# Splitting w_out into two parts during the last k, v and q projections, by way of a DRAM scratch

## The chip, the cores and the metric

The kernel runs on one core of one Trainium2 chip. The metric is the time of one execution on the device in microseconds; the figure before is the median of three runs. The profile is of one further execution. Engines are named as the profile names them: PE is TensorE (PEld its weight loads), DVE is VectorE, ACT is ScalarE, POOL is GpSimd, SP is the engine whose queue issues nearly all DMAs here. Times within an execution are counted from the start of the profile's span.

## The reference

One layer of an encoder for two sequences (256 and 2048 tokens, each with 16 meta tokens ahead; 1024 channels). One input projection is cut into attention (q, k, v, gate) and convolution (value, gate, SiLU gate); both results are gated, joined, and go through one output projection:

```python
h = rmsnorm(z, norm_w)
proj = jnp.einsum('bld,de->ble', h, w_in)
q, k, v, g_att, c_val, c_glu, g_conv = jnp.split(proj, SPLIT_IDX, axis=-1)
...
att = windowed_gqa(q, k, v, sink).reshape(B, L, W_ATT) * jax.nn.silu(g_att)
cnv = conformer_conv(c_val, c_glu, conv_w, conv_b, ln_w, ln_b) * jax.nn.silu(g_conv)
mixed = jnp.concatenate([att, cnv], axis=-1)
return z + jnp.einsum('ble,ed->bld', mixed, w_out)
```

Everything is float32. w_out is 1024 x 1024, 4 MB.

## The kernel before

**Precision.** Matmuls run in float32r. To keep float32 accuracy each operand is split into two parts: hi is the value cast to float32r, lo is the rest (value minus hi). A product takes three matmuls, hi by hi, hi by lo and lo by hi (PASSES, L125). The split of a tile is a cast on ACT and a subtraction on another engine.

**Phase one, the projections.** Tokens come in 18 blocks of 128 and in 6 groups of 3 blocks; the groups form two chunks (c = 0 and c = 1). w_in is cut into 11 units of 256 columns. For each chunk the units are run in the order of ORDER (L965): four convolution units, two gates of the convolution, two gates of attention, k and v together (kv_group), and two units of q (q_group). In chunk 0 a unit's weights are loaded raw into tiles with the tag wraw (pool sp, four buffers of 2 KB per partition), split, and the two parts are stored in the DRAM scratch wd; in chunk 1 units 2 and up are loaded from wd in two parts (L720 to L724). So the wraw buffers are last used early in chunk 1's weight preparation. The results of phase one go to DRAM scratches (qd, kd, vd, gd), the convolution with its LayerNorm (ln_block) runs beside it and ends in cd. A kv or q block is 24 matmuls (proj_te); its head norm takes the square sums on ACT (and DVE), the reciprocal root on POOL (rsqrt, L121), and its results are stored with store (L158), whose DMA is due two ticks later.

**Phase two, attention and the output projection.** It opens ahead of the last q unit of chunk 1 (L1048 to L1054): the right-hand pools wr, sp and cp are closed, and the pool ap takes their place (attention_open). The work is a list of slots (slot_step), 8 for each step s_; step s_ computes scores of block a = s_, the weighted sums of block s_ - 1 and the output projection of block s_ - 2. Thirteen slots (EARLY) are run between the nine q blocks of the last unit (spread), the rest in attention_rest. The stretch in which this pipeline starts, while no output projection runs yet, is called the fill below. load_ga and load_mix bring a block's gates and convolution (tiles ga, gc, cn); mix_conv multiplies cn by gc on POOL and splits the product for the output projection (mch, mcl).

**w_out.** It is used as eight tiles e of 128 x 1024, in the order of OUT_ORDER. They stay on chip for the whole of phase two in the place of the split inputs xh and xl (pool xp, three buffers each, one for each group of chunk 1): load_wo(n) gives tile n its place, three tiles' halves to a buffer. WO_AT (L59) puts the loads of n = 0 to 2 behind the last q blocks of group 3, of n = 3 to 5 behind group 4, and of the last two behind group 5. A tile is loaded raw in two halves of 512 columns (tag woraw, two buffers in ap) and two ticks later split into its place by split_wo: a cast on ACT, a subtraction on DVE.

**The order of work.** The program calls tick between pieces of projection work; later(k, f) puts f behind k ticks. A planner then places every instruction: it walks the program with a model of the engines' times and gives each engine its instruction order, in which program order is the priority. In phase two POOL (MAN1), and later POOL and PE (MAN2), keep the program's order; a few instructions are pinned (pin), among them the first transpose of q. On the chip each engine, and SP's queue, runs its list in order, and an instruction whose data is missing holds up all behind it.

Of the kernel before, what the change touches and what calls it, by code (L numbers as in the profile page):

```python
# [10 lines left out]
F32 = mybir.dt.float32  # L11
F32R = mybir.dt.float32r
BF16 = mybir.dt.bfloat16
AF = mybir.ActivationFunctionType
ALU = mybir.AluOpType
AX = mybir.AxisListType

P = 128
D = 1024
# [13 lines left out]
UW = 256  # L33
# [31 lines left out]
U_Q = [6, 7]  # L65
# [4 lines left out]
def blk_local(b):  # L70
    g = b // 3
    return g, (NM if g == 0 else 0) + P * (b % 3)
# [3 lines left out]
def hymba_kernel(  # L76
# [13 lines left out]
    nc = tc.nc  # L90

    const = ctx.enter_context(tc.tile_pool(name="const", bufs=1, side="left"))
    dram = ctx.enter_context(tc.tile_pool(name="dram", bufs=1, space=bass.MemoryType.DRAM))
# [7 lines left out]
    vmd = dram.tile([NM, 2 * P], F32, name="vmd")  # L101
    wd = dram.tile([11, 4, P, 4 * UW], F32, name="wd")
    cd = dram.tile([NB, P, 512], F32, name="cd")

    ident = const.tile([P, P], F32, name="ident")
    make_identity(nc, ident)
# [26 lines left out]
    def owe(ns):  # L133
        credit[0] -= ns

    def later(k, f):
        due.setdefault(clock[0] + k, []).append(f)
# [4 lines left out]
    def tick(ns):  # L142
        credit[0] += LOAD * ns
        if ln_q and ln_q[0][0]():
            ln_q.pop(0)[1]()
            credit[0] -= 800
        while credit[0] > 0 and (conv_q[0] or conv_q[1]):
            side[0] ^= 1
            q = conv_q[side[0]] or conv_q[1 - side[0]]
            cost, f = q.pop(0)  # L150
            credit[0] -= cost
            f()
        credit[0] = min(credit[0], 0.0)
        clock[0] += 1
        for f in due.pop(clock[0], []):
            f()

    def store(dst, src):  # L158
        later(2, lambda: nc.sync.dma_start(dst, src))
# [8 lines left out]
    sp = right_pools.enter_context(tc.tile_pool(name="sp", bufs=2, side="right"))  # L168
# [43 lines left out]
    pool, cst, kw, wo, wo_slot, sbs = {}, {}, [], {}, {}, []  # L212
    vt, qt, q2t, sbt, pmt, gat, gct, cnt, mix, att, yot, opj = ({} for _ in range(12))
    OUT_ORDER = (4, 5, 6, 7, 0, 1, 2, 3)
# [61 lines left out]
    def load_wo(n):  # L276

        e = OUT_ORDER[n]
        for hl in range(2):
            idx = 2 * n + hl  # L280
            if idx % 3 == 0:
                slot = idx // 3
                wo_slot[slot] = xp.tile([P, ND, 400], F32R, tag=("xh", "xl")[slot % 2], name=f"wo{slot}")
            flat = wo_slot[idx // 3].rearrange("p a n -> p (a n)")
            wo[e, hl] = flat[:, D * (idx % 3) : D * (idx % 3) + D]
        for nh in range(2):
            cols = slice(512 * nh, 512 * nh + 512)
            raw = pool["a"].tile([P, 512], F32, tag="woraw", name=f"woraw{n}_{nh}", bufs=2)
            nc.sync.dma_start(raw, w_out[e][:, cols])
            later(2, lambda hi=wo[e, 0][:, cols], lo=wo[e, 1][:, cols], raw=raw: split_wo(hi, lo, raw))  # L290

    def split_wo(hi, lo, raw):
        nc.scalar.copy(hi, raw)
        nc.vector.tensor_tensor(lo, raw, hi, op=ALU.subtract)  # L294

    def load_ga(b):
        gat[b] = pool["b"].tile([P, 4, P], F32, tag="ga", name=f"ga{b}", bufs=1)
# [319 lines left out]
    if True:  # L617
# [20 lines left out]
        class Prep:  # L638
# [50 lines left out]
            def split(self, d2):  # L689
                n, xt = self.n, self.xt[d2]  # L690
                xh, xl = xg[self.g]
                for dd in range(2):
                    d = 2 * d2 + dd
                    if self.pool:
                        nc.scalar.mul(xh[:, d, :n], xt[:, dd, :n], nw[:, d : d + 1])
                    else:
                        nc.scalar.copy(xh[:, d, :n], xt[:, dd, :n])  # L697
                for dd in range(2):
                    d = 2 * d2 + dd
                    if self.pool:  # L700
                        nc.vector.scalar_tensor_tensor(
                            xl[:, d, :n], xt[:, dd, :n], nw[:, d : d + 1], xh[:, d, :n], op0=ALU.mult, op1=ALU.subtract
                        )
                    else:
                        eng = nc.gpsimd if dd else nc.vector
                        eng.tensor_tensor(xl[:, d, :n], xt[:, dd, :n], xh[:, d, :n], op=ALU.subtract)  # L706
                owe(1000)
# [187 lines left out]
        def q_group(ws, qi, g, after):  # L895
            for b in range(3 * g, 3 * g + 3):
                ps = proj_te(ws, g, blk_local(b)[1], P)
                rq = head_norm(ps, P, 4, f"q{qi}_{b}")

                def fin(ps=ps, rq=rq, b=b):  # L900
                    qs = gp.tile([P, 4, HD], F32, tag="qs", name=f"qs{qi}_{b}")
                    nc.vector.tensor_tensor(  # L902
                        qs,
                        ps[:, :UW].rearrange("p (h e) -> p h e", e=HD),
                        rq.unsqueeze(2).to_broadcast([P, 4, HD]),
                        op=ALU.mult,
                    )
                    store(qd[b, :, UW * qi : UW * qi + UW], qs.rearrange("p h e -> p (h e)"))

                owe(340)  # L910
                later(1, fin)
                tick(24 * 110)
                after(b)
# [40 lines left out]

            later(1, fin)

        def kv_group(ws, g):
            if g == 0:
                kv_block(ws, 0, 0, NM, -1)
                tick(24 * 107)  # L960
            for b in range(3 * g, 3 * g + 3):
                kv_block(ws, g, blk_local(b)[1], P, b)
                tick(24 * 110)

        ORDER = U_C + U_GC + U_GA + [U_KV] + U_Q  # L965
        keys = [(c, u) for c in range(2) for u in ORDER]
# [80 lines left out]
        for i, (c, u, g) in enumerate(items):  # L1047
            if (c, u) == keys[-1] and g == CHUNKS[c][0]:  # L1048
                while conv_q[0] or conv_q[1]:
                    tick(3000)  # L1050
                for _ in range(3):
                    tick(0)
                right_pools.close()
                attention_open()  # L1054
            if u in U_C and g == CHUNKS[c][0]:
                u_tiles(c, u)
            ws = wsplit[c, u]
            at_item_start(i, c, u, g)
            for t, p, what in prep_at.get(i, []):
                if what == "load":  # L1060
                    for q in range(4):
                        later(1, lambda p=p, q=q: p.load(q))
                else:
                    later(1, p.first)
                    for q in range(4):
                        later(1 + q // 2, lambda p=p, q=q: p.scale(q))
            if u in U_C:
                c_group(c, u, ws, g)
            elif u in U_Q:
                q_group(ws, u - U_Q[0], g, spread if (c, u) == keys[-1] else lambda b: None)  # L1070
            elif u == U_KV:
                kv_group(ws, g)
            elif u in U_GC:
                g_group(ws, 4 + 2 * (u - U_GC[0]), g)
            else:
                g_group(ws, 2 * (u - U_GA[0]), g)
            for k in loads.get(i, []):
                load, split = weights(k)
                load(nc.sync)
                room = max(1, when[first_at[keys[k]]] - when[i + 1])  # L1080
                for q in range(4):
                    at = max(1, min(room, W0 + q * min(WST, max(1, (room - 2) // 4))))
                    later(at, lambda split=split, q=q: split(q, nc.vector))
            if c == 0 and u in U_GA:
                for k3 in range(3):
                    k = 10 + 3 * (3 * (u - U_GA[0]) + g) + k3
                    if k <= NB:
                        later(1 + k3, lambda k=k: later(1, stats(k)))
            if (c, u) == (0, ORDER[-1]):
                p = preps[g + 3]  # L1090
                p.alloc()
                for q in range(4):
                    later(1 + q // 2, lambda p=p, q=q: p.split(q))
            if u in U_C and g == CHUNKS[c][2]:
                conv(c, u, 0)
            if i == last_at[c, u] and u == U_GC[-1]:
                def ready(c=c):
                    if left[c, 0]:
                        return False
                    seen.setdefault(c, clock[0])  # L1100
                    return clock[0] >= seen[c] + LN_WAIT[c]

                for b in range(0, 8) if c == 0 else range(8, NB):
                    ln_block(c, b, ready)
# [60 lines left out]
```

## Time and profile before

| | |
|---|---|
| median of three runs | 979.26 us (978.87 to 979.48) |
| profiled execution, its own time | 981.45 us |
| span in the profile | 979.6 us |
| granted TensorE clock, mean | 0.994 |
| HBM read, written | 101.00 MB, 54.31 MB |

The span runs from the first to the last instruction; 1.85 us of the profiled execution's own time lie around it. The page divides the span into 40 slices of 24.5 us; a digit is the busy share in tenths. Queries on the trace answer with the same lines for any stretch: a window gives the busy time of each engine, the granted clock and the share of time in which the 16 DMA engines were busy; a line of waits names who waited, for whom, the total, the number and the longest; a line of a timeline gives start, duration, engine, line, operation and tiles (output, then inputs).

### The profile page before, as it was taken

To read this page: it belongs to the slowest core of one execution; us is meant where nothing else is said; L and a number is where in the kernel's file an instruction comes from. 1 tells how busy PE (TensorE), PEld (TensorE's weight loads), DVE (VectorE), ACT (ScalarE), POOL (GpSimd) and SP (SyncE) were. 2 spreads that over 40 slices of the span, in tenths; PEclk is the share of its full clock that TensorE was granted. 3 is DMA by queue.
4 is the path that set the end of the run, shared out by engine and by line. 5 is a ranking of instruction groups with operands and counts; after the bars stand their busy time and mean duration, and the time that the engine had idled before them with its cause. 6 is when DMAs were issued, how large, how long until landed. Compare 5 with 4: busy or idle time off the path is not lost.

```text
span 979.6 us, 16242 instructions
## 1 busy us (share of the span) xinstructions
PE 951.6 (97%) x5740; PEld 889.1 (91%) x5740; DVE 758.1 (77%) x1261; ACT 424.0 (43%) x1156; POOL 342.5 (35%) x541
## 2 busy tenths in 40 slices
PE   4999999999999999999999999799999999999998
PEld 4999999999999999999999999688888888888886
DVE  4749999988987699999983655977776777767772
ACT  5621122343467710111113445766666666566651
POOL 4600000373468300000002553645454454544451
PEclk9999999999999999999999999799999999999999
DMA  9643345785736222233335657954554455543321
GB/s 326 211 172 138 129 169 178 260 280 185 227 118 182 94 77 73 83 127 135 134 126 178 210 150 212 302 161 138 158 173 137 133 151 159 167 144 115 117 86 43
DMA packets 113872, 155.75 MB, mean 159 GB/s; under 512 B 10592, under 2 KB 77296, under 8 KB 113792
## 3 DMA queue, kind: packets, MB, share of 16 engines
q1 hardware_dynamic: 113648, 154.11, 48.0%
q0 software_dynamic: 144, 0.62, 0.4%
q8 instruction: 45, 0.74, 0.3%
q14 instruction: 35, 0.29, 0.1%
HBM read 101.00 MB, written 54.31 MB: 159 GB/s over the span
## 4 chain that ended last, share of the span: by engine, by line
PE 86%; DVE 5%; ACT 3%; DMA 3%; POOL 1%; issue 1%; SPq 1%; POOLq 0%; ACTq 0%
PE pj L766 41%; PE y L537 18%; PE pj L782 12%; PE pT L428 4%; PE O L463 4%; PE S L315 3%; DMA woraw<-in_w_out 1%; DVE q L338 1%; DVE q L337 1%; ACT q L336 1%; ACT q L335 1%; PE qT L315 1%; PE O L315 1%; DMA wraw<-in_w_in 1%; PE lnt L183 1%
## 5 line engine op out<-in xcount | busy, mean ns | idle before, releaser
L766 PE MATMUL pj<-xh,ws 128*128 128x384 f32 (+1 forms) x1536 | 397.0, 339 | 1.5 <-ACT xh L697 1.5
L849 DVE SCALAR_TENSOR_TENSOR y<-us,cw,y 128x1167 f32<-128x1167 f32 x240 | 328.9, 1428 | 0.6
L766 PEld LDWEIGHTS pj<-xh,ws 128*128 128x128 f32 x1536 | 282.0, 189 | 1.9 <-ACT xh L697 1.8
L766 PE MATMUL pj<-xl,ws 128*128 128x384 f32 (+1 forms) x768 | 262.2, 341 | 2.9 <-DVE xl L706 2.9
L782 PE MATMUL pj<-ws,xh 128*128 128x256 f32 (+1 forms) x880 | 163.7, 284 | 0.3 <-DVE qs L902 0.3
L766 PEld LDWEIGHTS pj<-xl,ws 128*128 128x128 f32 x768 | 144.8, 189 | 3.7 <-DVE xl L706 3.7
L782 PEld LDWEIGHTS pj<-ws,xh 128*128 128x128 f32 (+1 forms) x880 | 135.8, 187 | 0.8 <-DVE qs L902 0.5
L782 PE MATMUL pj<-ws,xl 128*128 128x256 f32 (+1 forms) x440 | 124.3, 283 | 0.0
L382 ACT ACTIVATE sb<-sb,nm 128x304 f32<-128x304 f32 (+4 forms) x144 | 77.1, 535 | 49.0 <-DVE nm L370 47.5
L537 PE MATMUL y<-wo,mch 128*128 128x512 f32 x288 | 96.7, 417 | 0.0
L537 PE MATMUL y<-wo,mah 128*128 128x512 f32 x288 | 93.6, 405 | 0.7 <-DVE wo L294 0.7
L440 DVE TENSOR_TENSOR pl<-pT,ph 128x512 fp32r<-128x512 f32 x100 | 68.9, 690 | 31.2 <-ACT ph L439 29.9
L874 ACT ACTIVATE go<-pj 128x384 f32<-128x384 f32 x48 | 23.6, 491 | 155.1 <-PE pj L766 145.6
L370 DVE CUSTOM_DVE_ANT_0 sb<-S,bias,nsnk 128x304 f32<-128x304 f32 (+4 forms) x144 | 73.2, 510 | 13.0 <-PE S L315 10.5
L782 PEld LDWEIGHTS pj<-ws,xl 128*128 128x128 f32 (+1 forms) x440 | 82.1, 187 | 0.2
L122 POOL TENSOR_SCALAR ssk<-ssk 128x2 f32<-128x2 f32 x18 | 6.4, 356 | 213.0 <-ACT sqk L888 212.9
L405 POOL TENSOR_SCALAR sb<-sb,es 128x304 f32<-128x304 f32 (+4 forms) x144 | 74.3, 535 | 3.6
L439 ACT CAST ph<-pT 128x512 fp32r<-128x512 f32 x100 | 58.2, 584 | 25.6 <-PE pT L428 24.4
L122 POOL TENSOR_SCALAR ssq<-ssq 128x4 f32<-128x4 f32 (+2 forms) x55 | 27.9, 507 | 115.0 <-ACT xn L631 76.6
L315 PEld LDWEIGHTS S<-kw,q 128*128 128x128 f32 x288 | 53.7, 191 | 15.5 <-DVE nm L370 3.5
L428 PE MATMUL pT<-ident,sb 128*128 128x128 f32 x400 | 62.1, 276 | 3.7 <-DVE q L338 3.5
L315 PE MATMUL S<-kw,q 128*128 128x304 f32 (+4 forms) x288 | 62.8, 300 | 2.5 <-DVE nm L370 2.4
(118 smaller groups left out, 1443.6 us busy)
## 6 DMA issues: line engine op xcount, KB each, us to landing
wd<-ws SPq DMA_DIRECT2D x36, 512.0 KB, 5.6
ws<-wd SPq DMA_DIRECT2D x36, 512.0 KB, 5.2
wraw<-in_w_in SPq DMA_DIRECT2D x52, 256.0 KB, 5.7
xn<-in_z SPq DMA_DIRECT2D x18, 512.0 KB, 5.5
gd<-go SPq DMA_DIRECT2D x48, 192.0 KB, 2.1
yo<-in_z SPq DMA_DIRECT2D x36, 256.0 KB, 2.6
out_y<-yo SPq DMA_DIRECT2D x36, 256.0 KB, 2.1
kw<-kd SPq DMA_DIRECT2D x16, 512.0 KB, 5.7
```

The costliest lines, as they stand in the source:

```text
L315: r = f(*a, **k)
L370: nc.vector.tensor_tensor_reduce(out=sb[:, n, c0:c1], in0=ps[:, 0:w], in1=cst["bias"][:, kv, n, c0 - QB * n : c1 - QB * n], scale=1.0, sca ...
L382: nc.scalar.activation(sb[:, n, c0:c1], sb[:, n, c0:c1], AF.Exp, bias=nm[:, n : n + 1], scale=-1.0, accum_out=rs[:, n : n + 1],)
L405: nc.gpsimd.tensor_scalar(sb[:, k, a0:a1], sb[:, k, a0:a1], es[:, k : k + 1], 1.0, op0=ALU.mult, op1=ALU.mult)
L428: nc.tensor.transpose(pt[:, hl, :], sbt[b, kv][:, hl, KCOL[k] : KCOL[k] + P], ident)
L439: nc.scalar.copy(ph, pt)
L440: nc.vector.tensor_tensor(pl, pt, ph, op=ALU.subtract)
L463: nc.tensor.matmul(o, lhs, t, start=(start and i == 0), stop=(stop and i == 1))
L537: nc.tensor.matmul(ps, mh[mi][:, e % 4, :], wo[e, wi][:, cols], start=(e == 4 and k == 0), stop=(e == 3 and k == 2),)
L766: nc.tensor.matmul(ps[:, :n], ws[:, d, wi, P * half_i : P * half_i + P], x[xi][:, d, o : o + n], start=(k == 0), stop=(k == 3 * ND - 1),)
L782: nc.tensor.matmul(ps[:rows, :UW], x[xi][:, d, o : o + rows], ws[:, d, wi, :], start=(k == 0), stop=(k == 3 * ND - 1),)
L849: nc.vector.scalar_tensor_tensor(y[:, yo + o0 : yo + o1], u[:, o0 + k : o1 + k], cw[:, j, k : k + 1], y[:, yo + o0 : yo + o1], op0=ALU.mul ...
```

## The change

w_out is split earlier, and its two parts go through DRAM. There is a new scratch wod (8 tiles, 2 parts, 128 x 1024). After each block of chunk 1's kv unit (9 blocks) and after the first seven blocks of chunk 1's first q unit, split_next starts one of 16 halves of w_out tiles: a load of 256 KB into a wraw tile, and two ticks later a cast on ACT into another wraw tile, a subtraction on POOL in place, and two stores of 256 KB to wod, due two more ticks later. load_wo keeps its places and times; it now loads each part of a tile whole, 512 KB, from wod into its place, and splits nothing. The tag woraw is gone from ap.

```diff
+    wod = dram.tile([8, 2, P, D], F32, name="wod")
...
             wo[e, hl] = flat[:, D * (idx % 3) : D * (idx % 3) + D]
-        for nh in range(2):
-            cols = slice(512 * nh, 512 * nh + 512)
-            raw = pool["a"].tile([P, 512], F32, tag="woraw", name=f"woraw{n}_{nh}", bufs=2)
-            nc.sync.dma_start(raw, w_out[e][:, cols])
-            later(2, lambda hi=wo[e, 0][:, cols], lo=wo[e, 1][:, cols], raw=raw: split_wo(hi, lo, raw))
-
-    def split_wo(hi, lo, raw):
-        nc.scalar.copy(hi, raw)
-        nc.vector.tensor_tensor(lo, raw, hi, op=ALU.subtract)
+            nc.sync.dma_start(wo[e, hl].bitcast(F32), wod[e, hl])
+
+    def split_wo(m):
+
+        e, cols = OUT_ORDER[m // 2], slice(512 * (m % 2), 512 * (m % 2) + 512)
+        raw = sp.tile([P, 2, UW], F32, tag="wraw", name=f"woraw{m}", bufs=4)
+        nc.sync.dma_start(raw.rearrange("p a n -> p (a n)"), w_out[e][:, cols])
+
+        def split():
+            hi = sp.tile([P, 2, UW], F32R, tag="wraw", name=f"wohi{m}", bufs=4)
+            nc.scalar.copy(hi, raw)
+            nc.gpsimd.tensor_tensor(raw.bitcast(F32R), raw, hi, op=ALU.subtract)
+            store(wod[e, 0][:, cols], hi.rearrange("p a n -> p (a n)").bitcast(F32))
+            store(wod[e, 1][:, cols], raw.rearrange("p a n -> p (a n)"))
+
+        later(2, split)
...
+        wo_n = [0]
+
+        def split_next(b):
+            if wo_n[0] < 16:
+                split_wo(wo_n[0])
+            wo_n[0] += 1
+
-        def kv_group(ws, g):
+        def kv_group(ws, g, after):
...
                 tick(24 * 110)
+                after(b)
...
-                q_group(ws, u - U_Q[0], g, spread if (c, u) == keys[-1] else lambda b: None)
+                q_group(ws, u - U_Q[0], g, spread if (c, u) == keys[-1] else split_next if c == 1 else lambda b: None)
...
-                kv_group(ws, g)
+                kv_group(ws, g, split_next if c == 1 else lambda b: None)
```

## The prediction

> **What bounds the kernel now.** I read the page first (engine shares, then the slices), then the windows around the places that the change touches, then the waits in them.
>
> ```profile
> span 979.6 us, 16242 instructions
> PE 951.6 (97%) x5740; PEld 889.1 (91%) x5740; DVE 758.1 (77%) x1261; ACT 424.0 (43%) x1156; POOL 342.5 (35%) x541
> ...
> PE   4999999999999999999999999799999999999998
> ...
> PEclk9999999999999999999999999799999999999999
> ```
>
> TensorE is busy for 951.6 of 979.6 us; everything else hides behind it. A change elsewhere can only act where TensorE has gaps or a lower clock, and both show in one slice, around 625 us. The windows give its price (columns: stretch, its length, busy us of PE, PEld, DVE, ACT, POOL, granted clock, DMA share, GB/s):
>
> ```profile
> 170.00:222.00 52.00, 52.00 (x298) 52.00 (x297) 47.88 (x40) 19.92 (x39) 25.42 (x20) 1.00 0.74 260
> 517.30:582.00 64.70, 64.70 (x557) 64.70 (x556) 35.16 (x77) 28.46 (x101) 30.69 (x85) 1.00 0.56 177
> 582.00:588.50 6.50, 4.53 (x40) 4.33 (x39) 1.56 (x5) 1.78 (x5) 2.12 (x5) 1.00 1.00 265
> 588.00:610.00 22.00, 20.54 (x169) 19.84 (x169) 12.01 (x36) 10.91 (x28) 8.76 (x16) 1.00 0.71 216
> 610.00:628.00 18.00, 13.68 (x68) 10.12 (x67) 16.56 (x46) 14.91 (x42) 12.53 (x19) 0.88 0.89 276
> 588.50:645.00 56.50, 49.36 (x305) 42.40 (x303) 43.09 (x110) 37.33 (x96) 29.75 (x45) 0.91 0.78 240
> 628.70:648.00 19.30, 18.62 (x86) 15.42 (x87) 16.76 (x40) 12.43 (x30) 11.75 (x16) 0.87 0.66 214
> 645.00:960.00 315.00, 312.58 (x1681) 263.26 (x1680) 226.60 (x588) 190.86 (x493) 155.10 (x239) 1.00 0.46 139
> ```
>
> From 517.3 to 582 us (last k, v and first q projections) TensorE has no gap. From 588.5 to 645, the **fill** of the attention pipeline, it idles 56.5 - 49.36 = 7.1 us, and at clock 0.91 its busy time loses another 49.36 x 0.09 = 4.4. These 11.6 us are the ceiling of any gain; after 645 TensorE is 99% busy. Who held it up:
>
> ```profile
> PE qT L315 <- DMA q<-qd: 2.0, 1, 2.0
> PE S L315 <- DVE nm L370: 2.4, 4, 1.4
> PE y L537 <- DVE mcl L520: 1.3, 1, 1.3
> PE y L537 <- DVE wo L294: 0.7, 1, 0.7
> ACT wo L293 <- DMA woraw<-in_w_out: 10.1, 8, 4.4
> DVE wo L294 <- ACT wo L293: 6.7, 5, 4.9
> ```
>
> The first wait is at the opening of attention (window 578 to 590), the others are of the fill. TensorE rarely waits for the w_out tiles themselves; it waits for scores and mixes that queue on VectorE (16.56 of 18 us busy from 610 to 628) behind the w_out splits and behind the raw loads that these wait for.
>
> **The change part by part.** Columns: count, busy us, mean ns, idle before; for L289 min/median/max ns of an issue, first and last; a wait of the SP queue; for DMA issues count, KB each, us to landing; two windows.
>
> ```profile
> L293 ACT CAST wo<-woraw 128x512 fp32r<-128x512 f32 x16 | 9.9, 618 | 10.3 <-DMA woraw<-in_w_out 10.1
> L294 DVE TENSOR_TENSOR wo<-woraw,wo 128x512 fp32r<-128x512 f32 x16 | 13.2, 827 | 7.0 <-ACT wo L293 6.7
> L742 POOL TENSOR_TENSOR ws<-wraw,ws 128x512 fp32r<-128x512 f32 x4 | 5.7, 1430 | 2.9 <-ACT ws L741 2.9
> woraw<-in_w_out SPq DMA_DIRECT2D x16, 256.0 KB, 3.7
> L289 SPq DMA_DIRECT2D woraw<-in_w_out x16: 327/333/564, 595.4 to 640.5; - x16
> SPq L289 <- DVE wo L294: 11.2, 8, 2.8
> wd<-ws SPq DMA_DIRECT2D x36, 512.0 KB, 5.6
> kd<-ks SPq DMA_DIRECT2D x18, 256.0 KB, 2.6
> 552.00:556.00 4.00, 4.00 (x37) 4.00 (x36) 2.49 (x6) 1.43 (x5) 1.59 (x4) 1.00 1.09 375
> 628.00:632.00 4.00, 3.32 (x11) 2.94 (x12) 3.96 (x8) 1.92 (x5) 2.48 (x4) 0.50 1.06 368
> ```
>
> *Removed from the fill*: 16 VectorE subtractions (13.2 us) and 16 ScalarE casts (9.9 us), with the 6.7 and 10.1 us that these engines stood still for them. Between nothing and the 11.6 us ceiling, depending on what ends last then.
>
> *Added before it* (517 to 582): the same 16 casts on ScalarE, 28.46 + 9.9 = 38.4 of 64.7 us; 16 subtractions on GpSimd at 1430 ns (the same shape, L742), 30.69 + 22.9 = 53.6 of 64.7. Both still fit. A cast that waits for its raw load blocks the head norms behind it on ScalarE, and a late subtraction blocks their rsqrt on GpSimd and, through its two stores, the SP queue; the four PSUM buffers of the projections cover that for some blocks (18 blocks in the 61 us from 517.3 to 578.5, 3.4 us each). I charge 1 us; without the cover it is at most the 10.1 us that the same casts wait today. The SP queue gets 48 more issues, 16 us at 333 ns, beside 64.7.
>
> *Added traffic there*: 16 x (256 KB in + 512 KB out) = 12.6 MB. The best 4 us windows carry 368 and 375 GB/s with the DMA engines full, so 12.6 MB / 370 = 34.0 us. Free are (1 - 0.56) x 64.7 = 28.5 us, and the first 3 or 4 cannot be used, since a raw load starts only after the first block. So the stores **overrun** 582 us by 5.5 to 9 us, into a stretch with DMA share 1.00. There stands the load that TensorE already waits for:
>
> ```profile
> 578.54 0.79 POOL L226 DMA_DIRECT2D bias<-in_bias_c  x1
> ...
> 579.50 2.44 SPq L242 DMA_DIRECT2D kw<-kmd  x2
> 581.98 0.98 SPq L274 DMA_DIRECT2D q<-qd  x1
> ...
> 617.36 0.42 SPq L304 DMA_DIRECT2D cn<-cd  x1
> ...
> 621.59 1.28 POOL L514 TENSOR_TENSOR cn<-cn,gc 128x512 f32<-128x512 f32 x1
> ...
> 628.68 0.79 PE L537 MATMUL y<-wo,mcl 128*128 128x512 f32 x1 [1.32 <-DVE mcl L520]
> ```
>
> At most the four wraw buffers can be in flight, 4 x 256 KB = 1.05 MB or about 3 us, ahead of q<-qd: the 2.0 us wait becomes 5. Besides, the buffers of the raw tiles lie in memory that attention takes over; a kw load into such a place stands on SP until the last store has landed, about 588 to 591, where L242 is issued at 579.5 today. The first scores then come 0 to 9 us late, of which the remaining q blocks on TensorE hide most. Both together: +5 (from 0 to 12).
>
> *The fill's own traffic*: 16 loads of 512 KB in place of 16 of 256 KB. They no longer wait on SP for a raw buffer (11.2 us today) but for the last projection that reads the xh or xl in whose place they go; behind them queue the loads of q, k, gc and cn. From 588 to 628 the DMA engines work 0.71 x 22 + 0.89 x 18 = 31.6 of 40 us. Take out the 12 of 16 raw loads issued by then (3.15 MB, 8.5 us) and put in 8.4 MB (22.7 us): 45.8. About 2.6 MB in it (x rows 1.05, block 1's gate and conv tiles 0.5, block 3's q and k 1.05) may come later, 7 us. So 38.8 us must still pass before the tiles of block 0's mix are there, since gc and cn of block 0 are issued behind the last w_out tiles: about 627, then GpSimd's product (1.28) and ScalarE's cast (0.6), and the first output matmuls start near 629, as now (628.68). The engines are freed, but the transfer is late in their place. After that point the present run loses 19.3 - 18.62 = 0.7 idle and 18.62 x 0.13 = 2.4 to the clock up to 648; that I give to the change: -3 (from -11.6 to +3).
>
> Sum: 1 + 5 - 3 = **+3 us** on the profiled execution, which took 981.45 us (span 979.6, 1.85 around it). The median of the runs shown is 979.26, 2.2 below, so the forecast is 979.26 + 3 = **982.3 us**.
>
> Here a page speaks the other way. The Trainium skill, "HBM Reference", section Access, says that a core streaming alone gets about 425 GB/s. By it, as an estimate, the added 12.6 MB take 29.6 us and fit nearly into the free time, and the overrun, and with it the +5, goes. No 4 us window here passes 375. What would follow is rival 1, worked out from rows of its own.
>
> **The rivals.**
>
> 1. *The fill is freed* (faster). If the w_out stores keep pace with the projections (for it: from 170 to 222 us, at 260 GB/s of the same loads, splits and stores, TensorE lacks nothing) and the last four w_out loads do not hold up block 0's cn, TensorE is the only limit of the fill. It then gets back some 60% of 11.6, 7 us: 972.3. It speaks against it that the fill's DMA share is already 0.89 from 610 to 628. It decides at a cn landing before about 622.
> 2. *One cancels the other* (same): the overrun is hidden by the q projections and the fill merely changes from a VectorE limit to a DMA limit, 979.3. For it: only one wait of 2.0 us on a q load is on TensorE's path today.
> 3. *Attention opens late* (clearly slower, the far part of my forecast's side): the four buffers go through load, cast, subtraction and store, 3.7 + 0.6 + 1.4 + 5.6 = 11.3 us for a raw buffer and 0.6 + 5.6 = 6.2 for a cast one, 17.5 us of buffer per half, 4.4 us per half with four buffers. 16 halves from 521 end at 591, and stores in a full queue end later. If kd stores lengthen too (2.6 us now, two buffers), ScalarE's k cast waits. With the gain of 3 lost as well: +8, 987.3.
>
> **How the numbers follow.** Forecast 0.36, rival 1 0.35, rival 2 0.17, rival 3 0.12. By sign (0.2%, 2 us, is about what can be told from no change) rival 1 is faster, rival 2 the same, and of the forecast's own range, 980 to 986, a tenth falls below +2: faster 0.35, same 0.21, slower 0.44. Both signs hold much, since the gain and the two losses come from the same 50 us of DMA time. The range takes in most of rival 1 down to 970.5 (three quarters of the ceiling) and rival 3 up to 989.
>
> **What would show it.** Right: in 517 to 588 us a DMA share near 0.9 or above, the last wod store landing after 586, TensorE's wait for qT above 4 us, and the first output matmul not before 627 with its wait on mch or cn, or on wo loads. Rival 1: the slice at 625 us shows 9 for PE and clock, VectorE falls below 14 us in 610 to 628, and the first output matmul comes before 622. Wrong altogether: a different order of instructions after 645 us, since the planner may place everything anew, or gaps on TensorE between 517 and 578.

## The result and the profile after

The changed kernel takes 987.72 us (median of four runs, 985.34 to 988.89) against 979.37 for the kernel before: a ratio of 1.0083, with a 95% interval from 1.0067 to 1.0099, or 8.3 us more. The prediction was 982.3, slower, with a range from 970.5 to 989.

The profiled execution took 988.89 us with a span of 987.1, 7.5 more than before. First its page, with the slices as before:

```profile
span 987.1 us, 16328 instructions
...
PE   5999999999999899999999999499999999999998
...
PEclk9999999999999999999999999699999999999999
DMA  9643345775736676233335659944554445543321
```

TensorE now has two weak places. The one near 625 us is deeper (4 in place of 7), and a new one, an 8, stands near 335 us, in the middle of the second chunk's first projections, where the change seemed to do nothing. The DMA row says why to look there. The same row of the page before was

```profile
DMA  9643345785736222233335657954554455543321
```

and in the three slices from 321 us on it now reads 6 7 6 where it read 2 2 2. The splits are there (rows of the tile woraw: minimum, median and maximum in ns, then the first and the last start):

```profile
L297 ACT CAST wohi<-woraw x16: 617/622/657, 317.7 to 383.6; 128x512 fp32r<-128x512 f32 x16
L298 POOL TENSOR_TENSOR woraw<-woraw,wohi x16: 1268/1295/2486, 318.4 to 384.3; 128x512 fp32r<-128x512 f32 x16
L160 SPq DMA_DIRECT2D wod<-woraw x16: 319/366/843, 319.7 to 386.9; - x16
```

The loads of the fill, as the rows of the tile wod have them, start 212 us after the last store:

```profile
L287 SPq DMA_DIRECT2D wo<-wod x16: 320/426/1196, 598.6 to 623.6; - x16
```

The program calls for the splits beside the last k, v and q projections, after 521 us here. The planner only takes program order as a priority: a raw load needs nothing but a free wraw buffer, so it put all sixteen splits some 200 us earlier, as soon as the last raw weights had left the buffers. The windows, with the columns as before:

```profile
330.00:340.00 10.00, 7.16 (x40) 6.62 (x39) 3.16 (x7) 5.91 (x11) 6.61 (x10) 0.89 0.70 250
517.30:582.00 64.70, 64.70 (x545) 64.70 (x545) 38.01 (x77) 26.47 (x96) 26.78 (x62) 1.00 0.51 170
588.50:645.00 56.50, 41.13 (x281) 36.55 (x280) 29.42 (x86) 26.23 (x73) 25.70 (x43) 0.85 0.95 331
628.70:648.00 19.30, 12.28 (x54) 9.95 (x55) 7.41 (x15) 5.19 (x14) 9.20 (x11) 0.67 0.80 257
610.00:628.00 18.00, 11.40 (x75) 8.98 (x73) 12.65 (x40) 10.30 (x30) 8.62 (x16) 0.90 1.04 387
```

From 517 to 582 us nothing is added at all. In the fill VectorE is indeed relieved (12.65 us from 610 to 628, 16.56 before), but the DMA engines are full, and TensorE loses 15.4 us there instead of 7.1. The waits of TensorE over the whole execution (microseconds in total, times, longest):

```profile
PE y L545 <- ACT mch L527: 13.0, 1, 13.0
...
PE lnu L203 <- DVE zn L197: 2.8, 2, 2.0
...
PE qT L323 <- DMA q<-qd: 1.1, 1, 1.1
```

The same view for VectorE, GpSimd and ScalarE, from 310 to 350 us:

```profile
POOL woraw L298 <- ACT wohi L297: 12.7, 6, 3.2
DVE zn L197 <- POOL mv L190: 12.0, 4, 5.3
...
ACT wohi L297 <- DMA wod<-wohi: 2.6, 1, 2.6
```

And for GpSimd from 596 to 645 us:

```profile
POOL cn L522 <- DMA cn<-cd: 11.5, 1, 11.5
```

The last of the three lines of the early place is a cast that waits on ScalarE for a wraw buffer whose store has not landed. It starts at 338.00 us, too late for TensorE's gap; the same chain two casts earlier leads into it. The timelines have it piece by piece, and the view of DMA issues from 328 to 329 us has the landing of the store, 3.2 us after its issue:

```profile
328.20 0.38 SPq L160 DMA_DIRECT2D wod<-wohi  x1
wod<-wohi SPq DMA_DIRECT2D x1, 256.0 KB, 3.2
331.50 0.62 ACT L297 CAST wohi<-woraw 128x512 fp32r<-128x512 f32 x1 [1.47 <-POOL xl L714]
332.20 1.28 POOL L298 TENSOR_TENSOR woraw<-woraw,wohi 128x512 fp32r<-128x512 f32 x1 [1.36 <-ACT wohi L297]
335.06 0.81 DVE L197 TENSOR_SCALAR zn<-lnt,mv 128x512 f32<-128x512 f32 x1 [4.27 <-POOL mv L190]
335.92 0.66 PE L203 MATMUL lnu<-ident,zn 128*128 128x128 f32 x4 [2.00 <-DVE zn L197]
```

The profile puts the cast's wait down to xl, but xl was done 0.7 us before the cast; the store landed at 331.43, 0.07 us before it. GpSimd stands in its fixed order at the subtraction behind the cast; the small LayerNorm instructions (mv) come after that on GpSimd; VectorE's zn waits for mv, and TensorE's transpose of zn waits for that. TensorE's second wait, 0.8 us at 338.03, needs no late store: there mv stands behind a subtraction of 1.27 us that waited for nothing. In the late place there is one wait of 13 us, for block 0's product of convolution and gate. The chain that ended last shows what it waited for:

```profile
614.06 10.94 DMA kw<-kd
625.01 0.37 SPq L306
625.42 7.51 DMA gc<-gd
632.98 0.69 issue
633.70 1.27 POOL cn L522
635.00 0.63 ACT mch L527
```

A load of k issued at 614 lands 10.9 us later and gc after 7.5, in the same stretch as the 8.4 MB of w_out. Four points of time sum it up. The first matmul of the k and v unit starts at 517.14 us before and 521.18 after, +4.0; the last matmul of the q projections at 613.04 and 613.93, +0.9, so 3.1 us are regained; the first output matmul at 626.50 and 635.67, +9.2 (the first with mcl, which is the one that the prediction reads, at 628.68 and 636.94, +8.3); the last output matmul at 975.41 and 982.50, +7.1.

### The profile page after: what moved, and what is told of

The parts are those of the page before. It is cut to its first block, busy times and chain, and to the rows that moved or that the text cites. A ratio compares the mean times of both kernels' runs of the same rounds, so it can differ in the third digit from the quotient of the medians.

```text
span 987.1 us, 16328 instructions
## 1 busy us (share of the span) xinstructions
PE 951.0 (96%) x5740; PEld 889.8 (90%) x5740; DVE 755.8 (77%) x1245; ACT 424.3 (43%) x1156; POOL 364.6 (37%) x557
## 4 chain that ended last, share of the span: by engine, by line
PE 57%; DVE 3%; DMA 2%; ACT 2%; issue 1%; POOL 1%; SPq 0%; POOLq 0%
PE y L545 19%; PE pj L774 18%; PE pj L790 6%; PE pT L436 4%; PE O L471 4%; PE S L323 3%; DMA kw<-kd 1%; DVE q L346 1%; DVE q L345 1%; PE O L323 1%; PE qT L323 1%; ACT q L344 1%; ACT q L343 1%; DMA gc<-gd 1%; DMA q<-qd 1%
## 5 line engine op out<-in xcount | busy, mean ns | idle before, releaser
L857 DVE SCALAR_TENSOR_TENSOR y<-us,cw,y 128x1167 f32<-128x1167 f32 x240 | 335.9, 1454 | 0.6
L378 DVE CUSTOM_DVE_ANT_0 sb<-S,bias,nsnk 128x304 f32<-128x304 f32 (+4 forms) x144 | 73.4, 511 | 16.1 <-PE S L323 14.3
L545 PEld LDWEIGHTS y<-wo,mch 128*128 128x128 f32 x288 | 50.1, 193 | 20.0 <-ACT mch L527 13.3
```

Source lines behind the costliest of these rows:

```text
L378: nc.vector.tensor_tensor_reduce(out=sb[:, n, c0:c1], in0=ps[:, 0:w], in1=cst["bias"][:, kv, n, c0 - QB * n : c1 - QB * n], scale=1.0, sca ...
L545: nc.tensor.matmul(ps, mh[mi][:, e % 4, :], wo[e, wi][:, cols], start=(e == 4 and k == 0), stop=(e == 3 and k == 2),)
L857: nc.vector.scalar_tensor_tensor(y[:, yo + o0 : yo + o1], u[:, o0 + k : o1 + k], cw[:, j, k : k + 1], y[:, yo + o0 : yo + o1], op0=ALU.mul ...
```

## The experiments

Each ratio is against the kernel before, run on the same chip, with its 95% interval.

**Each half alone.** e2_split_only keeps the early splits and stores, but the fill loads raw and splits as before:

```diff
-            nc.sync.dma_start(wo[e, hl].bitcast(F32), wod[e, hl])
+        for nh in range(2):
+            cols = slice(512 * nh, 512 * nh + 512)
+            raw = pool["a"].tile([P, 512], F32, tag="woraw", name=f"worw{n}_{nh}", bufs=2)
+            nc.sync.dma_start(raw, w_out[e][:, cols])
+            later(2, lambda hi=wo[e, 0][:, cols], lo=wo[e, 1][:, cols], raw=raw: split_fill(hi, lo, raw))
```

> The early splits and the stores to wod stay, but the fill loads w_out raw and splits it as before, so wod is written and never read. Theory (the early splits cost TensorE about 4 us near 335 us, by ScalarE and GpSimd standing behind the stores): 983 to 985 us, with a gap of TensorE of about 3 us between 330 and 340 us. Rival (the fill's loads are the whole cost): 979 to 980 us.

It took 983.14 us, 1.0039 (1.0025 to 1.0054): 4.1 us, with a gap in the same place:

```profile
330.00:340.00 10.00, 7.94 (x49) 7.39 (x49) 2.41 (x4) 6.47 (x11) 5.79 (x10) 1.00 0.69 232
```

The gap is 2.1 us here, where 3 were expected; this trace does not show where the other 2 us go. e3_load_only has the loads without the splits:

```diff
-            nc.sync.dma_start(wo[e, hl].bitcast(F32), wod[e, hl])
+            nc.sync.dma_start(wo[e, hl].bitcast(F32), wd[2 + e, hl])
...
-            if wo_n[0] < 16:
+            if wo_n[0] < 0:
```

> No early split and no store; the fill loads 16 x 512 KB from the scratch wd (parts of w_in stand in for those of w_out, so the output is another one). Theory (the fill's traffic costs about 3 us net of the freed engines): 982 to 984 us, first output matmul about 8 us later than before. Rival (the splits are the whole cost, the fill gains): 973 to 979 us.

983.87 us, 1.0052 (1.0037 to 1.0067): 4.8 us. TensorE has no gap near 335 us (10.00 of 10), and the wait for mch is 14.3 us, with the first output matmul at 633.79. The two halves add to 4.1 + 4.8 = 8.9, the whole change cost 8.3: within the intervals, some 1.5 us to either side, there are these two costs and no third.

**Bytes.** e4_half_bytes loads only one part of each tile:

```diff
-            nc.sync.dma_start(wo[e, hl].bitcast(F32), wod[e, hl])
+            if hl == 0:
+                nc.sync.dma_start(wo[e, hl].bitcast(F32), wd[2 + e, hl])
+        wo[e, 1] = wo[e, 0]
```

> As the kernel with loads alone, but only one of the two parts of each tile is loaded and it serves as both parts (the output is another one): 8 x 512 KB, the bytes of before without the splits. Theory (bytes decide the fill): the first output matmul comes before 624 us, TensorE and clock keep 9 in the slice of 625 us, 971 to 976 us. Rival (the fill is held by the chain from scores to mix, not by bytes): 977 to 980 us.

973.01 us, 0.9936 (0.9921 to 0.9951): 6.1 us faster than before, with the same bytes of w_out as before, no split in the fill, and no load that waits on SP for a raw buffer. The first output matmul comes at 620.20 us, after a wait of 3.2 us. One item of the expectation missed: from 610 to 628 us TensorE is still not fully busy and its clock is lower.

```profile
610.00:628.00 18.00, 13.03 (x58) 9.54 (x56) 13.28 (x33) 10.32 (x28) 12.38 (x18) 0.81 1.07 352
```

So the freed engines and the freed queue are worth 6 us, about half of the 11.6 us ceiling, and the second 4.2 MB cost 983.87 - 973.01 = 10.9, nearly what the transfer takes by itself at 387 GB/s (10.8). In this order of loads the added bytes cost their whole time; e12_all_gates_early below carries the same bytes in another order and is only some 5 us above e4_half_bytes.

**Which load is late.** e1_gates_first loads the last two w_out tiles behind block 0's gates:

```diff
-                if WO_AT[n] == b // 3:
+                if WO_AT[n] == b // 3 and n < 6:
...
         load_ga(0)
         load_mix(0)
+        load_wo(6)
+        load_wo(7)
```

> The last two w_out tiles (n = 6 and 7, 2.1 MB) are loaded behind block 0's ga, gc and cn instead of ahead of them. Theory (the fill is held by block 0's gc and cn, which queue behind w_out): cn lands about 5.7 us earlier (2.1 MB at 370 GB/s), the first output matmul starts near 630 instead of 636.9 us, and the time falls to 982 to 984 us. Rival (the bytes bind in any order): TensorE then waits as long for the w_out tiles of e = 2 and 3, time 986 to 988 us.

984.53 us, 1.0051 (1.0036 to 1.0066): 3.2 us less than the change, but above the 982 to 984 of the theory. The planner let one of the four loads go ahead all the same, and the first output matmul still waits 9.2 us for mch, at 632.13. e5_early_mix gives gc and cn of block 0 tiles in ap, in the room that woraw left, and loads them when attention opens:

```diff
             nc.sync.dma_start(vm[r0 : r0 + NM].rearrange("p a e -> p (a e)").bitcast(F32), vmd)
+        load_mix(0)
...
+        if b == 0:
+            gct[b] = pool["a"].tile([P, 4, P], F32, tag="gc0", name=f"gc{b}", bufs=1)
+            cnt[b] = pool["a"].tile([P, 4, P], F32, tag="cn0", name=f"cn{b}", bufs=1)
...
         load_ga(0)
-        load_mix(0)
```

> The changed kernel, with gc and cn of block 0 in tiles of their own in the pool ap (the room that woraw left) and loaded when attention opens, ahead of all w_out loads. Theory (cn of block 0 behind the w_out loads is what holds the first output matmul): TensorE's wait on mch is gone, the output starts before 626 us, 978 to 981 us. Rival (the 8.4 MB bind whatever comes first): another late load, ga, kw or a w_out tile, takes its place and the time stays at 984 to 987 us.

982.31 us, 1.0034 (1.0021 to 1.0046), between the two forecasts; the ten runs spread from 980.28 to 985.31, and the profile is of the fastest. The wait for mch is gone, and another takes half of its place (waits of TensorE over the whole execution):

```profile
PE pT_m L440 <- POOL pm L411: 5.6, 1, 5.6
```

GpSimd's waits from 600 to 650 us have what stands behind it:

```profile
POOL at L519 <- DMA ga<-gd: 8.8, 1, 8.8
```

Now ga of block 0 is the late load; GpSimd stands at the product with it, and the transposes of the next block's meta weights wait behind. Order and bytes both count: cn was the load on the path, and next to it stood another one.

**Where the prediction had put the splits.** e6_pinned holds the raw loads to their place in the program:

```diff
-        nc.sync.dma_start(raw.rearrange("p a n -> p (a n)"), w_out[e][:, cols])
+        tc.keep_in_program_order(nc.sync.dma_start(raw.rearrange("p a n -> p (a n)"), w_out[e][:, cols]))
```

> The changed kernel with the 16 raw loads pinned to their place in the program, so that the splits run among the last k, v and first q blocks (517 to 582 us) instead of at 312 to 387 us. The prediction's step (12.6 MB overrun that stretch by 5.5 to 9 us and the opening of attention is late): DMA share near 0.9 there, TensorE's wait at qT 4 to 6 us, 986 to 990 us. Rival (there is room, and only the early place cost 4 us): 983 to 985 us.

1002.71 us, 1.0231 (1.0214 to 1.0248): 23 us, far above both forecasts. The windows:

```profile
517.30:600.00 82.70, 76.78 (x633) 75.31 (x633) 35.69 (x79) 37.64 (x123) 50.52 (x92) 0.98 0.87 291
600.00:660.00 60.00, 40.26 (x225) 33.76 (x224) 29.46 (x85) 24.32 (x68) 28.24 (x56) 0.83 0.96 318
```

SP's timeline, with start and duration first, has the last store of a split and the opening of attention behind it:

```profile
599.13 0.39 SPq L160 DMA_DIRECT2D wod<-woraw  x1
...
606.58 1.27 SPq L243 DMA_DIRECT2D kw<-kmd  x2
607.89 0.62 SPq L275 DMA_DIRECT2D q<-qd  x1
```

SP's waits from 595 to 612 us:

```profile
SPq L243 <- DMA wod<-woraw: 3.9, 1, 3.9
```

And TensorE's from 515 to 660 us:

```profile
PE pj L790 <- DVE qs L910: 7.4, 2, 6.8
```

ScalarE's and VectorE's from 515 to 612 us:

```profile
ACT wohi L297 <- DMA wod<-wohi: 18.3, 6, 4.4
DVE nsnk L240 <- DMA snk<-in_sink: 5.3, 1, 5.3
```

The overrun is there, DMA share 0.87, the last store issued at 599 us, and the kw load stands on SP until it has landed, with q behind it, 26 us later than the 581.98 of the kernel before. Two things cost TensorE time. From 517 to 600 us it idles 82.7 - 76.8 = 5.9 us (2.0 in the kernel before), while the casts wait 18.3 us for stores to land. Then the late opening: the wait of TensorE for q that was expected to grow to 4 to 6 us does not appear, but a small load of the opening, snk, is late as well; VectorE stands 5.3 us for it, qs comes behind that at 611.04, and TensorE waits 6.8 us for qs. If the fill costs its 4.8 us (e3_load_only) here too, the place costs some 18, so the planner's early place was the cheaper one.

**What makes the early gap.** e9_no_stores is e2_split_only without the stores:

```diff
-            store(wod[e, 0][:, cols], hi.rearrange("p a n -> p (a n)").bitcast(F32))
-            store(wod[e, 1][:, cols], raw.rearrange("p a n -> p (a n)"))
```

> e2_split_only without the 32 stores to wod: the early loads, casts and subtractions stay, their results are dropped, and the fill loads and splits w_out as before. Theory (ScalarE's casts stand for buffers whose stores have not landed, and the LayerNorm chain behind them on ScalarE and GpSimd makes the gap of TensorE at 330 to 340 us): the gap goes, 979 to 980.5 us. Rival (the casts and subtractions themselves crowd ScalarE and GpSimd there): the gap stays, 982 to 984 us.

978.77 us, 1.0005 (0.9992 to 1.0018), and TensorE is whole again:

```profile
330.00:340.00 10.00, 9.95 (x63) 9.56 (x62) 4.39 (x9) 6.68 (x16) 6.92 (x14) 1.00 0.52 157
```

Without stores the casts and subtractions cost nothing, though GpSimd is even busier in that window than in e2_split_only and zn still waits for mv, 7.0 us from 310 to 350 instead of 12.0. The stores, and the buffers that they hold, turn that delay into a gap. Whether the wait for a buffer alone does it, or also the other order of instructions that the planner makes with the stores, this run does not separate; more buffers would, but there was no memory for them.

**Another place.** e7_conv_stage calls and pins the splits one at each projection item of chunk 1's later convolution and gate units, 366 us and later, after the first chunk's LayerNorm:

```diff
+            if c == 1 and u in (2, 3, 4, 5, 9, 10):
+                split_next(0)
```

> The splits called and pinned one by one at the starts of the projection items of chunk 1 from the third convolution unit to the last gate (about 370 to 510 us), where GpSimd is idle and ScalarE nearly so. Theory (splits cost only where they stand in front of the LayerNorm chain): no gap of TensorE in 320 to 517 us, 983 to 985 us, the fill unchanged. Rival (the stores or GpSimd slow VectorE's convolution wherever they are): 986 us or more.

1058.69 us, 1.0805 (1.0789 to 1.0821): 79 us, a forecast that missed altogether. GpSimd's timeline has one subtraction:

```profile
424.44 86.00 POOL L298 TENSOR_TENSOR woraw<-woraw,wohi 128x512 fp32r<-128x512 f32 x1 [16.25 <-ACT wohi L297]
```

ScalarE's timeline, where the last bracket is the idle time ahead and what ended it:

```profile
516.76 0.62 ACT L297 CAST wohi<-woraw 128x512 fp32r<-128x512 f32 x1 [89.19 <-DMA woraw<-in_w_out]
```

TensorE's waits over the whole execution:

```profile
PE pj L774 <- ACT go L882: 73.9, 1, 73.9
```

SP's from 420 to 520 us:

```profile
SPq L160 <- POOL woraw L298: 87.1, 3, 85.2
```

And VectorE's group of that time (count, busy time, mean ns, idle time before):

```profile
L857 DVE SCALAR_TENSOR_TENSOR y<-us,cw,y 128x1167 f32<-128x1167 f32 x65 | 88.5, 1448 | 0.0
```

One subtraction took 86 us on GpSimd while VectorE ran 65 convolution taps (the multiply-adds of the convolution) without a pause. The store of its result stood on SP, the next raw load behind it, the next cast behind that on ScalarE, the gate activations behind the cast, and so the PSUM buffers for TensorE: 73.9 us. That store was issued at 510.47, right at the subtraction's end, so the 86 us are no error of the profile. e10_conv_vector moves the subtraction and nothing else:

```diff
-            nc.gpsimd.tensor_tensor(raw.bitcast(F32R), raw, hi, op=ALU.subtract)
+            nc.vector.tensor_tensor(raw.bitcast(F32R), raw, hi, op=ALU.subtract)
```

> e7_conv_stage with the 16 subtractions on VectorE instead of GpSimd. Theory (the 74 us gap of e7_conv_stage came from one GpSimd subtraction that took 86 us beside VectorE's unbroken taps, and SP's stores and loads behind it): no gap of TensorE before the fill, about 11 us more on VectorE hidden there, 983 to 985 us (the fill's cost alone). Rival (the pinned loads on SP are the fault): above 1000 us.

983.30 us, 1.0040 (1.0025 to 1.0055). TensorE is busy for all of the 197 us from 320 to 517, and VectorE hides the 16 x 0.69 = 11 us:

```profile
320.00:517.00 197.00, 197.00 (x1135) 196.88 (x1134) 177.59 (x159) 42.69 (x82) 6.32 (x13) 1.00 0.47 168
```

The early half of the change is then free, and what is left agrees with e3_load_only.

**Everything together.** e8_conv_early_mix joined e5_early_mix to e7_conv_stage before the fault of the latter was known:

> e7_conv_stage and e5_early_mix together. If both costs are understood and add up: 973 to 977 us, faster than the kernel before. If the bytes bind in the fill: 980 to 984 us.

1053.58 us, 1.0749 (1.0733 to 1.0765); beside the 79 us it says that the early gates again save some 5 us, and the long subtraction is there again, 85.90 us beside the same 65 taps. e11_gates_ahead joins e10_conv_vector, e5_early_mix and e1_gates_first:

> e10_conv_vector with block 0's gc and cn loaded at the opening of attention (as in e5_early_mix) and the last two w_out tiles behind block 0's ga (as in e1_gates_first). If the early splits are free and the fill's cost is the order of its loads: 975 to 979 us. If the bytes of the fill hold it whatever the order: 980 to 983 us.

978.15 us, 0.9994 (0.9984 to 1.0005). e12_all_gates_early also loads ga of block 0 at the opening, in room that a fifth buffer of v had:

```diff
+        load_ga(0)
...
-        vt[b] = pool["a"].tile([P, KV, P], F32R, tag="v", name=f"v{b}", bufs=5)
+        vt[b] = pool["a"].tile([P, KV, P], F32R, tag="v", name=f"v{b}", bufs=4)
...
-        gat[b] = pool["b"].tile([P, 4, P], F32, tag="ga", name=f"ga{b}", bufs=1)
+        gat[b] = pool["a"].tile([P, 4, P], F32, tag="ga0", name=f"ga{b}", bufs=1) if b == 0 else pool["b"].tile([P, 4, P], F32, tag="ga", name=f"ga{b}", bufs=1)
```

> e11_gates_ahead with ga of block 0 at the opening too, in a tile of its own in ap (one v buffer fewer, 4 instead of 5, makes the room). Order of loads decides: 973 to 977 us, and faster than the kernel before. Bytes decide: the wait moves on to the gates of block 1, kw or a w_out tile, 979 to 982 us.

977.59 us, 0.9990 (0.9980 to 1.0000). The time that the change lost is regained, but neither version is shown to be faster than the kernel before. In e12_all_gates_early the DMA share from 610 to 628 us is still 1.06, and its waits from 600 to 650 us are

```profile
POOL pm L412 <- DVE es L411: 9.1, 2, 6.6
...
PE pT_m L441 <- POOL pm L412: 5.9, 1, 5.9
POOL cn L530 <- DMA cn<-cd: 4.7, 1, 4.7
```

TensorE waits for pm as in e5_early_mix; GpSimd itself now waits for VectorE's es, and for one more load of cn. None of these orders reached the 6 us of e4_half_bytes with 8.4 MB in that place.

## Why the prediction was right in sign, and where its steps failed

The sign and the range held; the size was 8.3 us where 3 was forecast. All three terms of the sum were off: 1 became about 4, 5 did not occur, and -3 became +4.8. That the range held is in part luck, since the 5 us that did not occur made up for about half of what the other two had too little. Of the four signs that the prediction named for being right, only the late first output matmul with its wait on mch came: the DMA share from 517 to 582 us was 0.51, the last wod store was issued at 386.9, and TensorE waited 1.1 us for q.

- *"517 to 582 ... I charge 1 us" for ScalarE and GpSimd*: the step that failed. It took the program's place of a split for its place in time. The planner had moved the work to 312 to 387 us, and there it cost 4.1 (e2_split_only). In the program's place it would have been too small as well: in e6_pinned TensorE idles 5.9 us from 517 to 600 us, against 2.0 in the kernel before. The mechanism that the step named, casts and subtractions that hold up what stands behind them on ScalarE and GpSimd, was the right one; the cover differed: in the changed kernel behind them stood not the head norms with their PSUM buffers but the LayerNorm chain into TensorE. The text had listed a planner that "may place everything anew" among what would prove it wrong, yet no term had a bound for it.
- *"The overrun ... +5"*: did not happen in the changed kernel, where TensorE's wait for q fell from 2.0 to 1.1 us. In the place that the step assumed it does happen (e6_pinned), with one of the two waits that it named: kw stands on SP for the last store, but TensorE then waits for qs behind the late snk, not for q. That run is 23 us slower; of the 18 estimated for this place, some 12 remain without the 5.9 us up to 600, which is the upper bound of this term. Rival 3, whose 987.3 us is close to the time measured, rests on the same late opening: the number agrees, the mechanism does not.
- *"The engines are freed, but the transfer is late in their place"*: right, by e3_load_only and e4_half_bytes, and the transfer is the one that was named, gc and cn of block 0 behind the last w_out tiles. The term was mis-sized: -3 was forecast, within -11.6 to +3, and +4.8 measured, so beyond the upper bound. The sum put cn at 627 by filling the DMA engines from 588 us on without a gap. In fact the w_out loads begin at 598.6 us, the share from 588 to 610 is 0.89, and SP can issue gc only at 625.4, behind the w_out issues, which themselves wait until earlier w_out loads have landed:

```profile
SPq L287 <- DMA wo<-wod: 4.7, 4, 2.0
```

  The first output matmul then starts at 635.67. The 3 us that were credited for the stretch from 628.7 to 648 were not gained either: TensorE is busy for 12.28 of its 19.3 us at a clock of 0.67, where it was 18.62 and 0.87 before.
- *Rival 1* had the right price for freed engines: 7 us, and e4_half_bytes gained 6.1. It decided against itself just where it said: cn would have had to land by 622, and GpSimd's product of it starts at 633.70.
- *The rate*: "No 4 us window here passes 375" does not hold; in the kernel before, in the stretch from 170 to 222 us that rival 1 cites, there is

```profile
214.00:218.00 4.00, 4.00 (x25) 4.00 (x24) 4.00 (x4) 1.53 (x3) 3.69 (x4) 1.00 1.03 411
```

  The Trainium skill, "HBM Reference", section "Specifications (TRN2)" (not "Access", where the prediction has it), has a core alone at about 425 GB/s; this window comes near it. In the changed kernel the stretch from 610 to 628 us carries 387 GB/s with a DMA share of 1.04, more than the 370 used, and yet the transfer was late: the rate was not what failed.

## What to carry to other kernels

Before moving work off a busy engine by passing its result through DRAM, look whether the stretch that reads it back has DMA time free: here the share was 0.89 before the change, and 4.2 MB more cost 10.9 us, all of their transfer time, where the relieved engines gave 6. Where a planner orders the instructions, look up in its order where the new work really stands before pricing it, and ask there what is behind each new wait on the same engine and in the same DMA queue. In a full queue the small load that the next stage needs first (here 0.5 MB of gates) belongs ahead of the large one; that regained 5 of the 8 us.

## What the runs showed of the hardware

A subtraction of 128x512 on GpSimd, 1.3 us where VectorE leaves it alone, took 86 us beside 65 VectorE taps that followed each other without a pause. The taps of that stretch (minimum, median and maximum in ns) were not held up, but for the last, which began at 509.4 us, where the subtraction came to its end:

```profile
L857 DVE SCALAR_TENSOR_TENSOR y<-us,cw,y x65: 1427/1435/2317, 423.2 to 509.4; 128x1167 f32<-128x1167 f32 x65
```

Other subtractions beside taps came through much sooner. In the changed kernel they took up to 2.5 us, and a tap beside each of them took 1.7 to 2.5 instead of 1.43: either engine can be the one that is held up. One at 376.13 us of e7_conv_stage took 2.4 us beside two taps without a pause between them, so an unbroken run of taps alone does not make the long wait. What does, these traces do not show. The Trainium skill, "SBUF — State Buffer", section "SBUF: two separate sides", says that GpSimd and a VectorE operation with two SBUF inputs lock each other out of a shared port pair for a whole instruction; these rows agree with that, and go further: the one that waits was not served between one tap and the next, for some sixty of them. That it was this lock is an inference; what the runs show is that the same subtraction on VectorE, in the same place, removes the stall.
